# Layer 1's decode value rows: from split weights to raw float32 weights in four column groups

## The chip, the cores and the metric

The kernel runs on one core of one Trainium2 chip. The core has a matrix engine (PE in the profile; its weight loads are listed apart as PEld), a vector engine (DVE), a scalar engine (ACT), a general-purpose engine (POOL) and a queue that only issues DMAs (SP). [...] The metric is device time in microseconds (us), the median of several executions.

## The reference, cut to what matters

One inference step of two layers: a retention layer ("layer 1" here) and a sliding-window attention layer, for a prompt of 1024 positions and for 8 decode rows (one new token for each of 8 sequences). The change touches one product of layer 1, the value projection of the 8 decode rows:

```python
def retention_layer(x, S0, g_norm, w_in, g_out, w_out):
    B, L, _ = x.shape
    h = rmsnorm(x, g_norm)
    proj = h @ w_in                       # w_in: 1024 x 6144
    q, k, v, gate = jnp.split(proj, [RET_QK, 2 * RET_QK, 2 * RET_QK + RET_V], axis=-1)
    ...
    o, S = retention_scan(q, k, v, S0)    # S_t = gamma_h S_{t-1} + k_t^T v_t,  o_t = q_t S_t
    o = rmsnorm(o, g_out.reshape(RET_HEADS, RET_DV)).reshape(B, L, RET_V)
    o = o * jax.nn.silu(gate)
    return x + o @ w_out, S.astype(S0.dtype)
```

There are four heads, each with 512 value columns. So the product in question is, for each head, [8 x 1024] times [1024 x 512].

## The kernel before, in words

**The first stage** projects layer 1. The columns of the weight matrix are cut into 20 sets: for each head one query set and one key set of 256 columns and one value set of 512 columns, then eight gate sets of 256 columns. Each set is one matrix product of (prompt and decode rows) by (1024 x columns), done with a seven-product scheme of Strassen's kind: `SEQ7` names the seven weight operands A11, S2, S1, A12, S3, S4, A22, where the S are sums and differences of quarters of the weights. (The first two sets, the query and key sets of head 0, are done without the scheme.) Every product is done in a 3-term form: each operand is split into a high part in the type float32r (`hi`, `woh`, `xh`) and a remainder (`lo`, `wol`, `xl`), and hi*hi, hi*lo and lo*hi are added up in PSUM. `w_hi` (ACT, L216) and `w_lo` (DVE or POOL, L221) make the two weight parts, `w_sum` (POOL) the sums, from raw tiles of 128 x 1024 float32 (`raw`, five buffers, DMAs issued from ACT's queue, L181). A raw tile of a value set holds two blocks of 128 rows of the weights by 512 columns; four of them make a set.

**The order of work** is a plan: `prod_slot` makes one slot for each product and half of the prompt (`t` = 0, 1), so 14 slots for a set, each with an estimated time; their sum is a planned clock. PE's queue is the list of slots. The work of the other engines is put between slots in two ways: `later(n, ...)` at slot number n (evacuations of PSUM, spills to DRAM), and `when(t, ...)` at a planned time (raw loads, `w_sum`, `w_hi`, `w_lo` some microseconds before the product that needs them, and the steps of the decode rows' retention).

**Where the 8 decode rows go.** For query, key and gate sets the decode rows travel as two more columns of the moving operand (258 columns instead of 256). For value sets the weights are the moving operand and the prompt's positions the stationary one, so the decode rows have a product of their own, `vdec` (L334 to L344): the stationary operand is `xdecr` (the high parts of the 8 rows in columns 0 to 7, their remainders in columns 32 to 39) or `xdecd` (the same of a difference of two halves of the rows), 40 columns wide, the moving operand `woh` and then `wol` of A11, A12, S1 and A22, 256 columns each. Four times a value set, behind the slot with `t` = 1 of products 0, 2, 3 and 6, eight matmuls follow, into the PSUM tile `vd`. After the set `vout1` (ACT, L697) copies partitions 32 to 39 of `vd` into a ring buffer, `vout2` (DVE, L701) adds partitions 0 to 7, and SP writes the 8 x 512 values to the DRAM scratch `vscr` (L705). `xdec2_` and `xdec3_` (L502 to L508, four DVE operations and one POOL operation) prepare `xdecr` and `xdecd` while the first two sets run.

**The decode rows' retention.** From 10 us (planned) after the end of a value set, `dec_load` brings a piece of the recurrent state (L253) and the values from `vscr` to all partitions (L255), `dec_kv`, `dec_st`, `dec_y0`, `dec_y1` update it on ACT and DVE, and `dec_mm` (L277) sums over partitions on PE: four plain float32 matmuls with a stationary operand of 32 columns, each into its own 32 partitions of the PSUM tile `od`.

**After the first stage** come the chunked retention of the prompt (from L859 on), layer 1's output projection, and layer 2.

Of the kernel before, what the change touches and what calls it, by code (L numbers as in the profile page):

```python
# [7 lines left out]
F32 = mybir.dt.float32  # L8
# [8 lines left out]
ND = 8  # L17
# [53 lines left out]
def _trunk(ctx, tc, nc, a):  # L71
# [67 lines left out]
    xdecr = dcp.tile([128, 8, 40], F32R, name="xdecr")  # L139
    xdecd = dcp.tile([128, 4, 40], F32R, name="xdecd")  # L140
# [193 lines left out]
    def vdec(s, name):  # L334

        if name == "A11":
            s.pd = vdp.tile([128, 512], F32, name="vd")
        x, i, k0, first = {"A11": (xdecr, 0, 0, True), "A12": (xdecr, 0, 4, False),
                           "S1": (xdecr, 1, 0, True), "A22": (xdecd, 1, 0, False)}[name]
        dst = s.pd[0:40, 256 * i:256 * i + 256]  # L340
        for k in range(4):
            hi, lo = s.op[name, k // 2]
            mm(dst, x[:, k0 + k, :], hi[:, k % 2, :], start=(name == "A11" and k == 0), stop=False, skip_group_check=True)
            mm(dst, x[:, k0 + k, :], lo[:, k % 2, :], start=False, stop=(k == 3 and not first), skip_group_check=True)  # L344
# [57 lines left out]
    rdec = sp.tile([128, 8, ND], F32, name="rdec")  # L402
    rT = sp.tile([128, 7, 4, 4], F32, name="rT")
    rdif = sp.tile([128, 4, ND], F32, name="rdif")
# [95 lines left out]
    def xdec2_():  # L500

        dve.tensor_copy(xdecr[:, :, 0:8], rdec)  # L502
        dve.tensor_tensor(xdecr[:, :, 32:40], rdec, xdecr.bitcast(F32)[:, :, 0:8], SUB)
        pool.tensor_tensor(rdif, rdec[:, 4:8, :], rdec[:, 0:4, :], SUB)

    def xdec3_():
        dve.tensor_copy(xdecd[:, :, 0:8], rdif)
        dve.tensor_tensor(xdecd[:, :, 32:40], rdif, xdecd.bitcast(F32)[:, :, 0:8], SUB)  # L508

# [59 lines left out]
    def prod_slot(s, j, t):  # L569
        n = len(slots)  # L570
        name, x, b, first = SEQ7[j]
        dec = s.kind == "v" and t == 1 and j in (0, 2, 3, 6)

        def pe():
            if first:
                s.bk[b, t] = bank(b, t)
            product(s, s.bk[b, t], t, name, x, first)
            if dec:
                vdec(s, name)

        us = 2.84 if s.kind == "v" else 1.43
        slot((us + (0.95 if dec else 0.0)) * (1.045 if s is not sets[2] else 1.0), pe)
# [31 lines left out]
        [o(g1_open), o(th, T2, 5), o(t12, 7), o(tl, T2, 5), o(t34, 7), o(dsums, 0, (T4,)), o(xdec2_)],  # L614
        [o(th, T2, 7), o(th, T1, 5), o(tl, T2, 7), o(tl, T1, 5), o(xdec3_), o(dsums, 1, (T2,))],
# [1319 lines left out]
```

## Time and profile before

| | |
|---|---|
| median of 3 runs | 1350.39 us (1350.27 to 1351.85) |
| profiled execution, its own time | 1350.44 us |
| its span in the trace | 1348.6 us |
| granted PE clock, mean | 0.995 |
| busy: PE, PEld, DVE, ACT, POOL | 1308.8, 1222.4, 701.1, 633.6, 707.4 us |
| first stage's last product begins / chunked retention begins on PE | 539.7 us / 543.3 us |
| value sets of heads 0 to 3 begin on PE | 70.7, 155.6, 243.0, 330.5 us |

How to read the rows: a timeline row has the start, the duration, the engine, the line of the kernel, the operation, the tile written and the tiles read, the active part of the array (rows*columns), the shape, a count, and in brackets the idle time of the engine before it with what ended it. Matmuls overlap in a pipeline: one of 256 columns is shown as lasting 0.28 us, though the next one starts 0.12 us after it. So the cost of a matmul on PE is the distance between starts, not the duration. A plain float32 matmul leaves two records in the trace (64 such matmuls of `dec_mm` leave 128).

### The profile page before, as it was taken

What the parts mean: (1) busy time and instruction counts of PE and PEld (TensorE: products, weight loads), DVE (VectorE), ACT (ScalarE), POOL (GpSimd) and SP (SyncE); (2) the same over time, 40 slices, a digit from 0 to 9 for tenths busy, and PEclk for the clock granted to TensorE, in tenths of its full rate; (3) what the DMA queues carried; (4) which work ended last, traced back from release to release, by engine and by line L of the source; (5) the groups of instructions that cost most, each with busy time, mean ns of one, the idle gap of its engine ahead of it and who ended that gap; (6) DMA issues with size and microseconds to landing.
All of it is one profiled execution on the core that took longest, in us unless ns stands there. A gap on an engine that the chain in (4) does not pass through costs nothing.

```text
span 1348.6 us, 25951 instructions
## 1 busy us (share of the span) xinstructions
PE 1308.8 (97%) x9661; PEld 1222.4 (91%) x9661; DVE 701.1 (52%) x1365; ACT 633.6 (47%) x1565; POOL 707.4 (52%) x825
## 2 busy tenths in 40 slices
PE   6999999999999999899999999998999999999998
PEld 6999999999999999787877899997889999998998
DVE  6943655656566553676752113335456555669321
ACT  5532444544455553677751112235465656656321
POOL 6653534435435543698977545454375666555000
PEclk9999999999999999999999999999999999999999
DMA  6314777587676753556556434442121111113532
GB/s 221 103 55 140 218 222 225 161 242 233 187 237 187 233 177 107 169 171 212 182 160 196 153 121 136 143 119 72 38 62 44 48 46 46 34 34 107 159 86 80
DMA packets 194771, 187.68 MB, mean 139 GB/s; under 512 B 12645, under 2 KB 174493, under 8 KB 194629
## 3 DMA queue, kind: packets, MB, share of 16 engines
q1 hardware_dynamic: 156576, 147.29, 35.9%
q10 hardware_dynamic: 38068, 38.73, 9.1%
q8 instruction: 76, 1.25, 0.4%
q14 instruction: 51, 0.41, 0.1%
HBM read 129.61 MB, written 57.41 MB: 139 GB/s over the span
## 4 chain that ended last, share of the span: by engine, by line
PE 85%; DVE 5%; POOL 4%; issue 3%; DMA 2%; ACT 1%; ACTq 0%; SPq 0%; POOLq 0%; DVEq 0%
PE b L330 7%; PE b L332 7%; PE b L331 7%; PE pj L1132 7%; PE pj L1134 6%; PE pj L1133 6%; PE b L323 4%; PE b L324 4%; PE b L325 4%; PE tr L100 4%; PE pj L1181 4%; PE pj L1179 4%; PE pj L1180 4%; PE o L1600 2%; POOL wl L1122 1%
## 5 line engine op out<-in xcount | busy, mean ns | idle before, releaser
L330 PE MATMUL b<-xh,woh 128*128 128x258 f32 x784 | 223.3, 285 | 0.0
L332 PE MATMUL b<-xh,wol 128*128 128x258 f32 x784 | 221.6, 283 | 0.0
L331 PE MATMUL b<-xl,woh 128*128 128x258 f32 x784 | 221.2, 282 | 0.0
L1132 PE MATMUL pj<-A_hi,wh 128*128 128x384 f32 (+1 forms) x512 | 178.7, 349 | 0.0
L1134 PE MATMUL pj<-A_hi,wl 128*128 128x384 f32 (+1 forms) x512 | 165.2, 323 | 0.0
L1133 PE MATMUL pj<-A_lo,wh 128*128 128x384 f32 (+1 forms) x512 | 165.1, 323 | 0.0
L330 PEld LDWEIGHTS b<-xh,woh 128*128 128x128 f32 x784 | 148.0, 189 | 4.1 <-issue 2.5
L331 PEld LDWEIGHTS b<-xl,woh 128*128 128x128 f32 x784 | 148.8, 190 | 0.0
L332 PEld LDWEIGHTS b<-xh,wol 128*128 128x128 f32 x784 | 148.1, 189 | 0.0
L221 POOL TENSOR_TENSOR wol<-raw,woh 128x512 fp32r<-128x512 f32 x52 | 68.5, 1325 | 139.7 <-ACT woh L216 139.0
L1122 POOL TENSOR_TENSOR wl<-wr,wh 128x1024 fp32r<-128x1024 f32 (+1 forms) x60 | 114.2, 1913 | 40.2 <-DVE wh L1121 19.5
L324 PE MATMUL b<-wol,xh 128*128 128x256 f32 x448 | 126.1, 281 | 0.3 <-DVE wol L221 0.3
L323 PE MATMUL b<-woh,xh 128*128 128x256 f32 x448 | 126.3, 282 | 0.0
L325 PE MATMUL b<-woh,xl 128*128 128x256 f32 x448 | 125.7, 281 | 0.0
L1132 PEld LDWEIGHTS pj<-A_hi,wh 128*128 128x128 f32 x512 | 97.3, 190 | 10.1 <-issue 9.4
L1133 PEld LDWEIGHTS pj<-A_lo,wh 128*128 128x128 f32 x512 | 97.6, 191 | 0.0
L1134 PEld LDWEIGHTS pj<-A_hi,wl 128*128 128x128 f32 x512 | 97.0, 190 | 0.0
L1577 POOL TENSOR_TENSOR s<-s,sm 128x512 f32<-128x512 f32 x64 | 68.9, 1077 | 49.7 <-DVE sm L1576 47.8
L323 PEld LDWEIGHTS b<-woh,xh 128*128 128x128 f32 x448 | 84.4, 188 | 2.5 <-issue 1.2
L324 PEld LDWEIGHTS b<-wol,xh 128*128 128x128 f32 x448 | 84.3, 188 | 0.8 <-DVE wol L221 0.8
L325 PEld LDWEIGHTS b<-woh,xl 128*128 128x128 f32 x448 | 84.3, 188 | 0.0
L1569 ACT ACTIVATE s<-s,mx 128x257 f32<-128x257 f32 x128 | 64.3, 505 | 30.2 <-DVE mx L1567 26.4
(379 smaller groups left out, 3564.7 us busy)
## 6 DMA issues: line engine op xcount, KB each, us to landing
raw<-in_w_in_ret_dram ACTq DMA_DIRECT2D x44, 512.0 KB
st<-in_state_ret_dram SPq DMA_DIRECT2D x64, 256.0 KB
out_dram<-st SPq DMA_DIRECT2D x64, 256.0 KB
wr<-in_w_out_ret_dram SPq DMA_DIRECT2D x32, 512.0 KB
wr<-in_w_in_swa_dram SPq DMA_DIRECT2D x18, 512.0 KB
vb<-vscr SPq DMA_DIRECT2D x64, 128.0 KB
evp<-qks SPq DMA_DIRECT2D x32, 256.0 KB
evx<-vsc SPq DMA_DIRECT2D x32, 256.0 KB
```

The costliest lines, as they stand in the source:

```text
L221: eng.tensor_tensor(lo, src_of(s, name, sub), hi.bitcast(F32), SUB)
L323: mm(dst, xh, wh, start=a and i == 0, stop=False, skip_group_check=True)
L324: mm(dst, xh, wl, start=False, stop=False, skip_group_check=True)
L325: mm(dst, xl, wh, start=False, stop=z, skip_group_check=True)
L330: mm(dst, wh, xh, start=a, stop=False, **sg)
L331: mm(dst, wh, xl, start=False, stop=False, **sg)
L332: mm(dst, wl, xh, start=False, stop=z, **sg)
L1122: lo_eng[0].tensor_tensor(lo[:, js, :], raw[:, i:i + step, :], hi.bitcast(F32)[:, js, :], ALU.subtract)
L1132: mm(ps, hi[:, k, fs], xh[:, k, t0:t1], start=first and k == ks[0], stop=False)
L1133: mm(ps, hi[:, k, fs], xl[:, k, t0:t1], start=False, stop=False)
L1134: mm(ps, lo[:, k, fs], xh[:, k, t0:t1], start=False, stop=last and k == ks[-1])
L1577: nc.gpsimd.tensor_tensor(st[:, :, 0:256], st[:, :, 0:256], sm.unsqueeze(2).broadcast_to([128, 2, 256]), ALU.mult)
```

## The change

`vdec` is called once per value set, behind product 0 with `t` = 1, and no longer uses the split weights. It multiplies the 8 normalised decode rows in plain float32 (`rdec32`, 32 columns wide with 24 columns of zeros) by the raw weight tiles, 512 columns at a time. The eight blocks of 128 weight rows are eight matmuls. Block kt goes to the 32 partitions of `vd` that begin at 32 * (kt mod 4): blocks 0 to 3 start the four partial sums, blocks 4 to 7 are added to them. After the set the four partial sums (partitions 0 to 7, 32 to 39, 64 to 71, 96 to 103) are added on ACT and DVE: three copies and three additions instead of one of each. The write to `vscr` moves from slot n + 4 to n + 6 (n is the first slot of the next set). `xdecr`, `xdecd`, `rdif` and their five preparing operations go. The planned time of a value set's extra slots changes from four times 0.95 us to once 2.05 us, so all planned times behind it shift.

```diff
-    xdecr = dcp.tile([128, 8, 40], F32R, name="xdecr")
-    xdecd = dcp.tile([128, 4, 40], F32R, name="xdecd")
+    rdec32 = dcp.tile([128, 8, 32], F32, name="rdec")
+    rdec = rdec32[:, :, 0:ND]
...
-    def vdec(s, name):
-
-        if name == "A11":
-            s.pd = vdp.tile([128, 512], F32, name="vd")
-        x, i, k0, first = {"A11": (xdecr, 0, 0, True), "A12": (xdecr, 0, 4, False),
-                           "S1": (xdecr, 1, 0, True), "A22": (xdecd, 1, 0, False)}[name]
-        dst = s.pd[0:40, 256 * i:256 * i + 256]
-        for k in range(4):
-            hi, lo = s.op[name, k // 2]
-            mm(dst, x[:, k0 + k, :], hi[:, k % 2, :], start=(name == "A11" and k == 0), stop=False, skip_group_check=True)
-            mm(dst, x[:, k0 + k, :], lo[:, k % 2, :], start=False, stop=(k == 3 and not first), skip_group_check=True)
+    def vdec(s):
+
+        s.pd = vdp.tile([128, 512], F32, name="vd")
+        for kt in range(8):
+            j, sub, kk, g = kt // 4, kt % 4 // 2, kt % 2, kt % 4
+            mm(s.pd[32 * g:32 * g + 32, :], rdec32[:, kt, :], s.raw[2 * sub + j][:, kk, :], start=(kt < 4), stop=(kt >= 4))
+
+    def vsum1(s, g):
+        s.vt = ring("c")[0:ND, 0:512]
+        act(s.vt, s.pd[32 * g:32 * g + ND, :], AF.Copy)
+
+    def vsum2(s, g):
+        if g == 1:
+            s.vs = ring("w")[0:ND, 0:512]
+        dve.tensor_tensor(s.vs, s.pd[0:ND, :] if g == 1 else s.vs, s.vt, ADD)
...
-        dec = s.kind == "v" and t == 1 and j in (0, 2, 3, 6)
+        dec = s.kind == "v" and t == 1 and j == 0
...
-                vdec(s, name)
+                vdec(s)
...
-        slot((us + (0.95 if dec else 0.0)) * (1.045 if s is not sets[2] else 1.0), pe)
+        slot((us + (2.05 if dec else 0.0)) * (1.045 if s is not sets[2] else 1.0), pe)
...
-            later(n + 1, vout1)
-            later(n + 2, vout2)
-            later(n + 4, lambda s=s: nc.sync.dma_start(out=vscr[s.h], in_=s.vs))
+            for g in (1, 2, 3):
+                later(n + g, vsum1, s, g)
+                later(n + g + 1, vsum2, s, g)
+            later(n + 6, lambda s=s: nc.sync.dma_start(out=vscr[s.h], in_=s.vs))
```

On PE, behind the first product of head 0's value set (`b` is the product's PSUM tile, `woh` and `wol` the split weights), the queue had before:

```order
L325 MATMUL b_985<-woh,xl 128x256
L343 MATMUL vd<-woh,xdecr 40x256
L344 MATMUL vd<-wol,xdecr 40x256
L343 MATMUL vd<-woh,xdecr 40x256
L344 MATMUL vd<-wol,xdecr 40x256
L343 MATMUL vd<-woh,xdecr 40x256
L344 MATMUL vd<-wol,xdecr 40x256
L343 MATMUL vd<-woh,xdecr 40x256
L344 MATMUL vd<-wol,xdecr 40x256
L323 MATMUL b_1034<-woh,xh 128x256
```

and now has, at the same place:

```order
L324 MATMUL b_976<-wol,xh 128x256
L325 MATMUL b_976<-woh,xl 128x256
L339 MATMUL vd<-raw,rdec 32x512 x8
L323 MATMUL b_1025<-woh,xh 128x256
L324 MATMUL b_1025<-wol,xh 128x256
```

Eight matmuls of 256 columns became eight of 512; the three other groups of eight in the set are gone. In head 2 the eight stand directly ahead of a group of `dec_mm` (L277), with no full-width matmul between them.

On DVE, while the first two sets run and up to the first two `wol` of head 0's value set (L476, L486, L487 split the prompt's operands), the queue had before:

```order
L502 CAST xdecr<-rdec 128x8x8
L503 TENSOR_TENSOR xdecr<-rdec,xdecr 128x8x8
L476 TENSOR_TENSOR xl<-raw,xh 128x4x128
L476 TENSOR_TENSOR xl<-u,xh 128x4x128
L507 CAST xdecd<-rdif 128x4x8
L508 TENSOR_TENSOR xdecd<-rdif,xdecd 128x4x8
L486 CAST xh<-rT 128x4x2
L487 TENSOR_TENSOR xl<-rT,xh 128x4x2
```

and now has (the lines' numbers are two higher):

```order
L478 TENSOR_TENSOR xl<-raw,xh 128x4x128
L478 TENSOR_TENSOR xl<-u,xh 128x4x128
L488 CAST xh<-rT 128x4x2
L489 TENSOR_TENSOR xl<-rT,xh 128x4x2
L478 TENSOR_TENSOR xl<-raw,xh 128x4x128
```

Four operations went from ahead of those `wol`; the order of the others is the same.

On DVE at the start of head 1's query set (`evp`, `evx`, `evw` are ring buffers that take the evacuated products), the queue had before:

```order
L701 TENSOR_TENSOR evw<-vd,evc 8x512
L361 TENSOR_TENSOR evp<-b_1486,evp 128x258
L361 TENSOR_TENSOR evp<-b_1503,evp 128x258
L221 TENSOR_TENSOR wol<-s_1484,woh 128x512
L363 TENSOR_TENSOR evx<-b_1521,evp 128x258
```

and now has:

```order
L348 TENSOR_TENSOR evw<-vd,evc 8x512
L348 TENSOR_TENSOR evw<-evw,evc 8x512
L365 TENSOR_TENSOR evp<-b_1453,evp 128x258
L348 TENSOR_TENSOR evw<-evw,evc 8x512
L365 TENSOR_TENSOR evp<-b_1472,evp 128x258
L221 TENSOR_TENSOR wol<-s_1451,woh 128x512
```

Two more additions stand ahead of the next `wol`; on ACT two more copies (L343) stand among the evacuations of the same slots.

More of the change, by code (lines that the diff above doesn't have):

```diff
@@ L766, in _trunk @@
         pool.memset(oneh[:, r, r:r + 1], 1.0)
-    pool.memset(xdecr.bitcast(F32), 0.0)
-    pool.memset(xdecd.bitcast(F32), 0.0)
+    pool.memset(rdec32, 0.0)
     nc.scalar.dma_start(out=gb, in_=norm_ret[0].partition_broadcast(128))
```

19 lines of the change are left out of this document (2 added, 17 removed).

## The prediction

> **What bounds the kernel now.** I read the page first, then the windows table, the table of waits, and last the timeline at the lines that the change touches. The page has the span and PE's share of it:
>
> ```profile
> span 1348.6 us, 25951 instructions
> PE 1308.8 (97%) x9661; PEld 1222.4 (91%) x9661; DVE 701.1 (52%) x1365; ACT 633.6 (47%) x1565; POOL 707.4 (52%) x825
> ```
>
> PE is busy 97% of the span, but the share is a mean over stages; the change lies in the first stage. The windows table for the stretch from shortly after the first value set's start to the stage's end (length, busy time of PE, PEld, DVE, ACT and POOL with counts, granted clock):
>
> ```profile
> 78.00:543.00 465.00, 464.76 (x3916) 455.22 (x3913) 247.65 (x432) 214.96 (x470) 207.86 (x243) 1.00 0.63 190
> ```
>
> PE is busy for 464.76 of 465 us at full clock, the other engines about half. The table of waits, for PE in the same stretch, consists of its heading alone:
>
> ```profile
> engine line waited for: us in total, times, longest us
> ```
>
> So PE waits for nobody there. A matmul more or less in this stretch is time more or less, at the distance between starts. The decode rows' value product is such work. One group of eight, from the timeline of PE:
>
> ```profile
> 77.26 0.28 PE L343 MATMUL vd<-woh,xdecr 128*40 128x256 f32 x1
> 77.38 0.28 PE L344 MATMUL vd<-wol,xdecr 128*40 128x256 f32 x1
> ...
> 78.08 0.28 PE L344 MATMUL vd<-wol,xdecr 128*40 128x256 f32 x1
> 78.20 0.28 PE L323 MATMUL b<-woh,xh 128*128 128x256 f32 x1
> ```
>
> The group takes PE from 77.26 to 78.20: 0.94 us, or 0.1175 for each matmul of 256 columns, whatever the width of its weights.
>
> **The change: what goes on PE.** The groups by line, from the view of line 343:
>
> ```profile
> L343 PE MATMUL vd<-woh,xdecr x48: 276/281/283, 77.3 to 356.6; 128*40 128x256 f32 x48
> L343 PE MATMUL vd<-woh,xdecd x16: 278/279/284, 114.2 to 375.3; 128*40 128x256 f32 x16
> ```
>
> That is 64, and each has a partner on line 344: 128 matmuls, 16 groups of eight. 16 x 0.94 = 15.0 us leave PE, 3.76 for each of the four value sets. All 16 lie in the stretch without waits, or at its edge.
>
> **What comes on PE.** For each value set eight plain float32 matmuls, 32 weight columns, 512 moving columns, in four column groups. Before has nothing of this size, but it has the same form with 256 columns: `dec_mm`, four plain float32 matmuls into four 32-partition groups of one PSUM tile, each with a moving tile of its own. Its view by line, and then one call in the timeline:
>
> ```profile
> L277 PE MATMUL od<-yd,oneh x128: 379/391/403, 158.5 to 495.5; 128*32 128x256 f32 x128
> ```
>
> ```profile
> 158.29 0.28 PE L325 MATMUL b<-woh,xl 128*128 128x256 f32 x1
> 158.49 0.64 PE L277 MATMUL od<-yd,oneh 128*32 128x256 f32 x8
> 159.06 0.38 PE L323 MATMUL b<-woh,xh 128*128 128x256 f32 x1
> 159.28 0.28 PE L324 MATMUL b<-wol,xh 128*128 128x256 f32 x1
> ```
>
> Each float32 matmul leaves two records (passes, I will say), so the four leave eight. A record lasts 0.38 to 0.40 us, and all eight together last 0.64: the four groups run at the same time, and what is left is two rounds, one for each pass. The price of the whole call: from the L325 at 158.29 to the L324 at 159.28 are 0.99 us; without the call the two starts behind that L325 would take 2 x 0.1175 = 0.235. So 0.755 us.
>
> To carry this to 512 columns I have to split it into rounds and a fixed part. The price of a pass without column groups stands in the next stage, four records (two float32 matmuls) of 128 columns, with a float32r matmul of 512 columns ahead:
>
> ```profile
> 549.45 0.40 PE L924 MATMUL po<-vh,sTl 128*128 128x512 f32 x1
> 549.68 0.61 PE L859 MATMUL tr<-evp 128*128 128x128 f32 x4
> 550.13 0.38 PE L100 MATMUL tr<-ident,evp 128*128 128x128 f32 x2
> ```
>
> From 549.68 to 550.13 are 0.45 us for four: 0.1125 for 128 columns, so 0.225 for 256 and 0.45 for 512. Two rounds of 256 are 0.45; of the 0.755 there remain 0.305, which is the cost of going into the narrow groups and out again, once for a call. [...]
>
> For a value set: blocks 0 to 3 are two rounds, blocks 4 to 7, added to the same partitions, two more. 4 x 0.45 + 0.305 = 2.105 us; four sets 8.4 us. The gain on PE is 15.0 - 8.4 = 6.6 us. From both sides: a pass of 512 can be a little cheaper than four of 128 (L924's 512 columns take 0.23 where 256 take 0.1175, 1.96 times), which makes a round 0.44 and the four sets 0.16 us cheaper or more; the fixed part may be half as large (0.6 us cheaper over the sets) or twice as large (1.2 dearer). In head 2 the order puts a `dec_mm` right behind the eight, so one way in and one way out of the narrow groups can fall away together: between 0 and 0.3 us more; I take 0.15.
>
> **The start of the first value set.** There PE does wait, for the remainders `wol` of the first operand:
>
> ```profile
> 70.72 0.28 PE L323 MATMUL b<-woh,xh 128*128 128x256 f32 x1
> 71.33 0.39 PE L324 MATMUL b<-wol,xh 128*128 128x256 f32 x1 [0.34 <-DVE wol L221]
> 71.55 0.29 PE L325 MATMUL b<-woh,xl 128*128 128x256 f32 x1
> ...
> 72.74 0.28 PE L323 MATMUL b<-woh,xh 128*128 128x256 f32 x1
> 73.02 0.38 PE L324 MATMUL b<-wol,xh 128*128 128x256 f32 x1
> 73.25 0.28 PE L325 MATMUL b<-woh,xl 128*128 128x256 f32 x1
> ```
>
> Twice two steps of 0.1175 became longer: 0.83 - 0.235 and 0.51 - 0.235, together 0.87 us. The `wol` come late because DVE works through its queue without a gap up to them:
>
> ```profile
> 63.24 0.18 DVE L502 CAST xdecr<-rdec 128x64 fp32r<-128x64 f32 x1
> ...
> 63.60 0.69 DVE L476 TENSOR_TENSOR xl<-raw,xh 128x512 fp32r<-128x512 f32 x1
> ...
> 64.81 0.17 DVE L507 CAST xdecd<-rdif 128x32 fp32r<-128x32 f32 x1
> ...
> 65.13 1.19 DVE L486 CAST xh<-rT 128x8 fp32r<-128x8 f32 x1
> ...
> 68.08 0.16 DVE L486 CAST xh<-rT 128x8 fp32r<-128x8 f32 x1
> ...
> 70.59 2.38 DVE L221 TENSOR_TENSOR wol<-raw,woh 128x512 fp32r<-128x512 f32 x2
> ```
>
> The four operations that go took 63.60 - 63.24 = 0.36 and 65.13 - 64.81 = 0.32, so the `wol` can come 0.68 us earlier. How much of it arrives is not certain: the same L486 lasts 0.16 or 1.19 us, so DVE is slowed by something else here, and a shift can change that. Bounds: all 0.87 saved, or 0.3 lost; I take 0.5, near the 0.68.
>
> **The sums behind the set.** Two copies on ACT and two additions on DVE come on top in each head:
>
> ```profile
> L697 ACT ACTIVATE evc<-vd x4: 589/590/591, 115.3 to 375.8; 8x512 f32<-8x512 f32 x4
> L701 DVE TENSOR_TENSOR evw<-vd,evc x4: 672/672/677, 116.0 to 376.6; 8x512 f32<-8x512 f32 x4
> ```
>
> 2 x 0.59 + 2 x 0.67 = 2.5 us per head. I cost them at nothing on PE. The cover, at the start of head 1's query set: two DVE rows behind the new additions, an evacuation and a split, and the PE row that first needs that `wol` (fifth product of the set):
>
> ```profile
> 119.74 0.43 DVE L361 TENSOR_TENSOR evp<-b,evp 128x258 f32<-128x258 f32 x1 [3.09 <-PE b L332]
> 121.54 0.68 DVE L221 TENSOR_TENSOR wol<-s,woh 128x512 fp32r<-128x512 f32 x1
> 126.69 0.29 PE L330 MATMUL b<-xh,woh 128*128 128x258 f32 x1
> ```
>
> DVE stands idle for 3.09 us just where 1.34 us are added, and the `wol` is ready at 122.22, 4.5 us before PE wants it. If that cover were gone, a head would cost up to 2.5 us.
>
> The write to `vscr` stands two slots later and behind three sums; SP's queue behind it holds `dec_load` of head 0 and the spills. SP's two rows and the first reader of the values on ACT:
>
> ```profile
> 116.67 0.29 SPq L705 DMA_DIRECT2D vscr<-evw  x1
> 118.28 0.40 SPq L255 DMA_DIRECT2D vb<-vscr  x1
> 130.07 0.90 ACT L260 ACTIVATE kv<-vb,kd 128x256 f32<-128x256 f32 x2
> ```
>
> The write may go some 3 to 4 us later (two query slots of about 1.45 us, and the sums), so `vb` is asked for at 122 instead of 118.28, and is wanted at 130: hidden. The other heads begin their decode steps later than 10 us after their set. Four of the eight matmuls wait for the DMA of a raw tile; the weight sums for the next product are planned 9 to 13 us ahead of it and read all four tiles, so these waits are over before PE comes to them. The raw tiles now have PE as one more reader, behind product 0; their last reader is still a sum on POOL for product 4 or a split for product 6, so the loads do not move for that.
>
> **Sum.** 6.6 + 0.15 + 0.5 = 7.25 us. The profiled execution took 1350.44 (0.05 above the median of the runs, so no correction): 1350.44 - 7.25 = 1343.2 us.
>
> **The rivals.** *Two passes in strict order (4%).* If a matmul's two passes stand one behind the other in PE's queue and no matmul starts before the one ahead of it, then a group overlaps only the second pass of one block with the first of the next: nine rounds for eight blocks, 9 x 0.45 + 0.305 = 4.36 us instead of 3.76, 2.4 us more over the sets, less the 0.65 of the two small terms: 1352.2. [...] Against it speaks the `od` row: in strict order its four would need five rounds, the last starting 4 x 0.225 = 0.9 us after the first, and the call would last 0.9 + 0.38 = 1.28 us instead of 0.64.
>
> *The groups do not overlap at 512 columns (4%, the other sign).* Four streams of 512 float32 into one PSUM tile could be held up where four of 256 from small tiles are not. With no overlap at all the eight cost 16 x 0.45 + 0.305 = 7.5 us, 3.74 more than now, 15.0 over the sets: 1350.44 + 15.0 - 0.65 = 1364.8. The point from which the change is a loss is 3.76 us for the eight, 7.7 rounds instead of 4. Nothing in the trace speaks for it; `od` fills a tile of four groups in the same way.
>
> *The gain is given back (6%).* PE arrives 7 us earlier at the end of the stage and could wait there for decode work or read-backs, giving 1350. Against it: the last `od` record starts at 495.5, and the next stage begins long after that:
>
> ```profile
> 543.33 0.68 PE L859 MATMUL tr<-evp 128*128 128x128 f32 x4 [0.56 <-issue]
> ```
>
> That is 48 us of slack for the decode rows, and the read-backs for the next stage are placed ten slots before the stage's end and move with it.
>
> **How the numbers follow.** A measurement of this kernel can tell about 0.2%, 2.7 us, from no change. The forecast has 86%. Its own range: 5.1 us of gain (fixed part doubled, 0.3 lost at the start, nothing in head 2) to 8.5 (rounds of 0.44, half the fixed part, 0.87 at the start, 0.3 in head 2): 1341.9 to 1345.3. The rivals hold 14%, so this range with 0.3 us of room on either side, 1341.6 to 1345.6, holds about 8 in 10. Faster by over 0.2%: 0.87 (the forecast, and a strong remainder of a partial give-back). Within 0.2%: 0.08 (strict order, most of the give-back). Slower: 0.05 (no overlap, or sums that surface).
>
> **What would show it.** In the new profile each value set should show one row of 16 records of `vd`, about 2.1 us from the last full-width start ahead to the normal rhythm behind; records of one round starting within some 0.03 us of one another, rounds 0.45 apart. The gap in front of the first `wol` of head 0 should be about gone. The table of waits for PE from 78 us to the stage's end should still be its heading alone, and the next stage should begin near 536. Starts of `vd` records spread evenly over 4 us or more would prove strict order or no overlap; rows of PE waiting for `wol` or `woh` in the query sets behind the value sets would prove that the sums are not hidden.

## The result, and the profile after

| | before | after |
|---|---|---|
| median (lowest to highest), 13 runs each, side by side | 1350.39 us (1348.51 to 1352.52) | 1347.49 us (1346.07 to 1349.89) |
| ratio, 95% interval | | 0.9978 (0.997 to 0.9987) |
| profiled execution, its span | 1350.44, 1348.6 us | 1346.37, 1344.6 us |
| retention begins on PE | 543.33 us | 535.78 us |
| from there to the end of the span | 805.28 us | 808.79 us |

The change gains 2.9 us where 7.25 were forecast, and the median lies 1.9 us above the range. In later comparisons the same two kernels are 5.2 and 6.6 us apart, so the gain is real and its size scatters. The last two rows of the table say where to look: the first stage became 7.55 us shorter, and the work behind it, which the change does not touch, 3.5 us longer.

The page of after, its span and its busy times:

```profile
span 1344.6 us, 25813 instructions
PE 1304.7 (97%) x9597; PEld 1213.1 (90%) x9597; DVE 709.6 (53%) x1369; ACT 636.2 (47%) x1573; POOL 710.1 (53%) x823
```

PE has 64 records fewer; that number returns below. The windows table of the first stage (length, busy time of PE, PEld, DVE, ACT, POOL with counts, granted clock, DMA share, GB/s):

```profile
70.00:78.00 8.00, 8.00 (x72) 7.24 (x74) 5.82 (x7) 4.46 (x9) 4.80 (x6) 1.00 0.07 19
78.00:536.00 458.00, 457.43 (x3854) 443.36 (x3843) 254.91 (x438) 218.57 (x479) 211.26 (x243) 1.00 0.64 193
```

PE is busy without a break, also from 70 to 78 us, where it waited before; the 0.57 us missing in the second row stand in front of the next stage. The table of waits for PE from 78 to 535.5 us is its heading alone again, so PE does not wait for the additional sums on ACT and DVE. The new product in the timeline of PE, head 0:

```profile
76.75 0.28 PE L325 MATMUL b<-woh,xl 128*128 128x256 f32 x1
76.96 1.92 PE L339 MATMUL vd<-raw,rdec 128*32 128x512 f32 x16
78.81 0.39 PE L323 MATMUL b<-woh,xh 128*128 128x256 f32 x1
79.04 0.28 PE L324 MATMUL b<-wol,xh 128*128 128x256 f32 x1
```

The sixteen passes together last 1.92 us. From the L325 at 76.75 to the L324 at 79.04 are 2.29 us; less two steps of 0.118, the set's decode product costs 2.05 us. And the first row of the next stage:

```profile
535.78 0.68 PE L843 MATMUL tr<-evp 128*128 128x128 f32 x4 [0.57 <-issue]
```

The stage came out close to the forecast (7.55 us for 7.25). What failed lies after 536 us, and in the time from which the gain was subtracted.

### The profile page after: what moved, and what is told of

It is laid out like the page before. It is cut to its first block, busy times and chain, and to the rows that moved or that the text cites. A ratio compares the mean times of both kernels' runs of the same rounds, so it can differ in the third digit from the quotient of the medians.

```text
span 1344.6 us, 25813 instructions
## 1 busy us (share of the span) xinstructions
PE 1304.7 (97%) x9597; PEld 1213.1 (90%) x9597; DVE 709.6 (53%) x1369; ACT 636.2 (47%) x1573; POOL 710.1 (53%) x823
## 4 chain that ended last, share of the span: by engine, by line
PE 86%; POOL 4%; DVE 3%; DMA 3%; issue 2%; ACT 2%; SPq 0%; ACTq 0%; POOLq 0%; DVEq 0%
PE b L330 7%; PE b L331 7%; PE b L332 7%; PE pj L1116 7%; PE pj L1117 6%; PE pj L1118 6%; PE b L323 4%; PE b L324 4%; PE b L325 4%; PE tr L100 4%; PE pj L1165 4%; PE pj L1163 4%; PE pj L1164 4%; PE o L1584 2%; PE b L537 2%
## 5 line engine op out<-in xcount | busy, mean ns | idle before, releaser
L324 PE MATMUL b<-wol,xh 128*128 128x256 f32 x448 | 126.0, 281 | 0.0
L325 PE MATMUL b<-woh,xl 128*128 128x256 f32 x448 | 125.6, 280 | 0.0
L325 PEld LDWEIGHTS b<-woh,xl 128*128 128x128 f32 x448 | 84.3, 188 | 0.0
L324 PEld LDWEIGHTS b<-wol,xh 128*128 128x128 f32 x448 | 84.3, 188 | 0.0
```

The lines of the kernel that those rows point to most:

```text
L324: mm(dst, xh, wl, start=False, stop=False, skip_group_check=True)
L325: mm(dst, xl, wh, start=False, stop=z, skip_group_check=True)
```

## Theories

**Theory A, blocks of instructions.** The trace lists among the DMA packets some of the kind "instruction", of 16 KB each in one queue:

```profile
q8 instruction: 76, 1.25, 0.4%
```

That is 76 packets for PE's 9597 records. Around 710 us they come 24 to 31 us apart, and between two of them PE has 113 to 129 matmul records; over the whole trace of after the middle value is 127 (91 to 163). So I take these to be PE's instructions, about 128 records (with their weight loads) in a block. The change takes 64 records out of PE's program, half a block, and every later packet falls half a block later in the work. Behind the first stage one of them then collides with a load that PE waits for.

**Theory B, the early arrival.** PE comes 7.5 us earlier to work whose loads do not come earlier by as much.

**Theory C, chance.** In the traces the granted clock falls to 0.50 for windows of 3.41 us, in other places in each execution: at 706.6, 921.6, 948.9 and 1259.5 us in before, at 698.9, 893.5, 910.6, 944.7 and, two in a row, 1006.1 us in after, and in both once more in the last microsecond. By this theory the forecast compared a lucky execution with ordinary ones.

The place for A and B: the stretch on PE from the first `S<-ident,xr` to the first `tr<-ident,kd`, layer 1's output projection and the beginning of layer 2. Before, then after:

```profile
706.70 1.09 PE L100 MATMUL S<-ident,xr 128*128 128x128 f32 x4 [3.12 <-DMA xr<-in_x_prompt_dram]
897.32 0.59 PE L100 MATMUL tr<-ident,kd 128*128 128x128 f32 x2 [0.15 <-DVE kd L1321]
```

```profile
698.88 1.04 PE L100 MATMUL S<-ident,xr 128*128 128x128 f32 x4 [3.03 <-DMA xr<-in_x_prompt_dram]
891.98 0.59 PE L100 MATMUL tr<-ident,kd 128*128 128x128 f32 x2 [1.00 <-DVE kd L1305]
```

It takes 190.62 us before and 193.10 after. Of the 3.5 us, 2.5 lie in this stretch and 1.3 behind it; ahead of it after is 0.3 us quicker. In the stretch PE waits for the remainder `wl` (POOL) of a projection weight; the chain behind it is `wh` (DVE) and the load of `wr` (issued by SP). Before, the timeline rows of that chain:

```profile
722.29 0.37 SPq L1114 DMA_DIRECT2D wr<-in_w_out_ret_dram  x1
726.06 1.11 DVE L1121 CAST wh<-wr 128x1024 fp32r<-128x1024 f32 x1 [2.67 <-DMA wr<-in_w_out_ret_dram]
729.69 0.50 PE L1181 MATMUL pj<-A_hi,wl 128*128 128x512 f32 x1 [0.46 <-POOL wl L1122]
```

and after:

```profile
714.30 0.37 SPq L1098 DMA_DIRECT2D wr<-in_w_out_ret_dram  x1
720.32 0.69 DVE L1105 CAST wh<-wr 128x1024 fp32r<-128x1024 f32 x1 [4.85 <-DMA wr<-in_w_out_ret_dram]
723.50 0.50 PE L1165 MATMUL pj<-A_hi,wl 128*128 128x512 f32 x1 [1.70 <-POOL wl L1106]
```

The same load comes 3.8 us after its issue before, and 6.0 us after it now; DVE waits for it 2.2 us longer and PE 1.2 us longer. The DMA view of after, first for 714.2 to 720.4 us, then for 717.9 to 719.1 us alone:

```profile
q8 instruction: 1, 0.02, 1.0%
```

```profile
DMA packets 71, 0.04 MB, mean 33 GB/s; under 512 B 10, under 2 KB 71, under 8 KB 71
```

One instruction packet lies between issue and landing (it starts at 717.15 us in the trace and lasts 0.95), and behind it the sixteen DMA engines together move 33 GB/s for 1.2 us, about a tenth of the 313 GB/s from 717 to 718 us: their busy share in the windows table falls from 1.02 to 0.14 while the rest of the load is still out. Before, the same view for 722.2 to 726.2 us has no instruction packet and a mean of 258 GB/s. Which of the sixteen engines were still at work is not shown.

The second place is 886 us, where SP and ACT issue small loads that the `kd` rows need. Before, then after:

```profile
891.89 0.81 SPq L1741 DMA_DIRECT2D xr<-xscr  x2
892.68 0.46 ACTq L1272 DMA_DIRECT2D kgb<-in_k_norm_dram  x1
```

```profile
885.97 1.82 SPq L1725 DMA_DIRECT2D xr<-xscr  x2
886.47 1.32 ACTq L1256 DMA_DIRECT2D kgb<-in_k_norm_dram  x1
```

In after an instruction packet starts at 886.38; the issues on both queues take 1.0 and 0.9 us longer, and PE waits 1.00 us for `kd` at the end of the stretch, where it waited 0.15 before.

## Experiments

Unless said otherwise, a run was timed beside the kernel before; the medians of before in these comparisons were 1351.43, 1352.35, 1353.26 and 1352.75 us.

**e1_before_again and e2_after_again** are the two kernels unchanged.

> The kernel before, unchanged, for a second trace and for the scatter of one against itself. The two traces at hand show the first stage shorter by 7.5 us (the chunked retention begins at 535.8 instead of 543.3), as the change's terms say, and the span shorter by 4.0 only: 3.5 us come back between 543 us and the end, where the two programs are the same. Theory chance: the part behind the first stage varies from execution to execution by a few us (half-speed windows of the granted clock, late DMAs), and the trace of before was a lucky one; then this trace has a first stage of 543.3 +-0.5 and a rest that differs from 805.3 us by 1 us or more, towards longer. Theory shift: the rest depends on when the first stage ends; then the rest is 805.3 +-0.7 again. The timed ratio is 1.000 +-0.001 by either.

> The changed kernel, unchanged, for a second trace. Theory chance: the first stage ends at 535.8 +-0.5, and the rest differs from the 808.8 us of its first trace by 1 us or more, towards shorter. Theory shift: the rest is 808.8 +-0.7 again. Ratio 0.998 by the runs so far.

Before: 1352.07 us, ratio 0.9999 (0.9989 to 1.001). After: 1346.23 us, ratio 0.9962 (0.995 to 0.9975). The retention began at 543.53 and 535.68 us, the stretch took 190.93 and 192.47 us. So both numbers belong to the kernels; the total gain, 5.2 us this time instead of 2.9, does so less. Nor does the whole rest from the start of the retention to the end of the span, on which the two expectations were built: it took 805.3 and 805.9 us in the profiles of before, 808.8 and 807.2 in those of after, and by itself the second value of after would have spoken for chance. That is why the stretch, and not the rest, is compared from here on.

**e3_product_twice** issues the new product twice for each value set.

```diff
-        s.pd = vdp.tile([128, 512], F32, name="vd")
+        if not hasattr(s, "pd"):
+            s.pd = vdp.tile([128, 512], F32, name="vd")
...
                 vdec(s)
+                vdec(s)
```

> The changed kernel with the eight column-group matmuls of each value set issued twice (the second eight compute the same values again). The second eight need no way in and out of the narrow groups, so they should cost four rounds of 0.43 us: 1.72 us a set, 6.9 in all, and the first stage should end at 542.7. Theory chance: the rest keeps its mean, the total is 1347.5 + 6.9 = 1354.4. Theory shift (what follows depends on when the first stage ends, and not on the kernel): the first stage ends where before's does, so the total is before's, 1350.4 +-0.7.

1351.78 us, ratio 1.0006 (0.9995 to 1.0017). The retention begins at 542.55 us, 6.8 us later than in the two profiles of after. In the timeline of PE:

```profile
76.94 3.64 PE L340 MATMUL vd<-raw,rdec 128*32 128x512 f32 x32
80.51 0.39 PE L323 MATMUL b<-woh,xh 128*128 128x256 f32 x1
```

The second product adds 3.64 - 1.92 = 1.72 us, four rounds of 0.43; the way into the narrow groups and out is paid once. The stage follows PE's work to a tenth of a microsecond. But the total rose by 5.5 us over e2, and the stretch went back to 190.93 us: the kernel has 9661 records again, like before.

**e4_before_half_product** leaves out half of the old decode product, two of its four groups of eight.

```diff
-            if dec:
+            if dec and j in (0, 2):
```

> The kernel before with two of the four groups of eight decode-row matmuls of each value set left out (those on A12 and A22, so half of each sum is missing from the decode rows' values); sums, evacuations, plan and everything else stay. PE has 64 matmuls of 0.1175 us less: the first stage should end at 543.3 - 7.5 = 535.8, as in the changed kernel. Theory chance: the rest keeps its mean, the total is 1350.4 - 7.5 = 1342.9. Theory shift: the total is the changed kernel's, 1347.5 +-0.7, since the first stage ends at the same time. Rival, the changed kernel's own doing (its rest is longer for something it does, not for the time at which it starts): 1342.9 here too, and 1354.4 with the product twice.

1348.26 us, ratio 0.9973 (0.9962 to 0.9984). The retention begins at 535.90 us, 7.4 earlier, for eight groups of 0.94. The stretch takes 192.90 us. So the longer stretch is not the new product's doing: this kernel, which does not have it, has 9597 records and an early retention too. A and B both allow that.

**e5, e6, e7 and e8** tell A from B. They put tiny matmuls into the time at the start in which PE waits for its first load (32 of them in e5 and e8, 64 in e6, 16 in e7; each leaves two records). The 64 of e6 last until 8.1 us, somewhat longer than that wait, but its first value set begins at 70.75 us, no later than the others.

```diff
+    pad = vdp.tile([128, 512], F32, tag="vd", name="pad")
+    for k in range(32):
+        mm(pad[0:32, 0:8], oneh[:, 0, :], oneh[:, 1, 0:8], start=True, stop=True)
```

In PE's timeline of e7 (16 matmuls) they end long before the load:

```profile
1.11 1.87 PE L772 MATMUL pad<-oneh 128*32 128x8 f32 x32 [1.11 <-POOL oneh L751]
7.33 0.99 PE L100 MATMUL pd<-ident,u 8*128 8x8 f32 x8 [4.35 <-DMA ident<-const_c_dram]
```

> The changed kernel with 32 tiny plain float32 matmuls (64 records, 8 columns each) put ahead of PE's first work; their result is overwritten unused. PE waits there until 7.5 us, so the retention should still begin on PE at 535.8 us. The stretch from the retention's last part to layer 2's norm (PE rows S<-ident,xr to tr<-ident,kd, near 700 to 890 us) took 190.6 to 190.9 us in the three runs with 9661 PE records and 192.5 to 193.1 in the three with 9597. Theory A, blocks of instructions: PE's instructions are fetched in packets of 16 KB (one every 128 records); 64 records fewer put one such packet between issue and landing of the wr load that PE waits for. 64 records more bring the packet back to where it was in the kernel before: 190.5 to 191.0 us, PE's gap at the wl wait 0.9 instead of 2.1, and a time 2 us below that of the changed kernel, 1344.5. Theory B, the earlier arrival itself collides with the loads: 192.5 to 193.1, 1346.5. Windows of half clock add 0 to 3 us to any single run.

> The same with 64 tiny matmuls, 128 records: one whole packet of instructions. Theory A: the packets fall on the same work as in the changed kernel, so the stretch is 192.5 to 193.1 us again and the time 1346.5, that is 2 us above the run with 64 records. Theory B: the same 192.5 to 193.1. A value near 190.7 would speak against both and for the extra records as such.

> The same with 16 tiny matmuls, 32 records: a quarter of a packet. Theory A: the packet that came at 717.1 us comes about 7 us earlier, near 710, ahead of the issue of the critical wr load at 714.3; the stretch is then 190.5 to 191.5 us and the time 1344.5 to 1345.5. Theory B: 192.5 to 193.1 and 1346.5.

> The kernel before with the same 32 tiny matmuls ahead, 64 records. The retention begins at 543.4 us as before. Theory A: the packet that came at 708.8 us comes near 695 and the next one near 723, between issue (722.3) and landing (726.1) of the wr load: the stretch becomes 192.5 to 193.1 us instead of 190.7 and the time 1352.5 to 1353.5, 2 us above the kernel before. Theory B: late arrival, so 190.6 to 190.9 and no change of time.

| | records | retention begins | packets in the stretch's first 40 us | stretch | median | ratio (95%) |
|---|---|---|---|---|---|---|
| e5, after + 64 | 9661 | 535.19 us | +2.1, +31.0 us | 191.21 us | 1345.76 us | 0.9951 (0.9939 to 0.9964) |
| e6, after + 128 | 9725 | 535.34 | +19.1 | 195.12 | 1347.43 | 0.9965 (0.9953 to 0.9977) |
| e7, after + 32 | 9629 | 535.56 | +11.8, +37.8 | 190.74 | 1344.07 | 0.9939 (0.9924 to 0.9954) |
| e8, before + 64 | 9725 | 543.28 | +17.9 | 194.04 | 1354.21 | 1.0011 (0.9999 to 1.0023) |

In the two profiles shown the packets come +18.3 us (after) and +2.1, +30.5 us (before) behind the start of the stretch. B falls: e5 and e7 begin the retention as early as after and have the short stretch, and e8 begins it as late as before and has the long one. A holds in all four, and e6, where a whole block was added, is long again. The clock, the other candidate, does not make the difference either: all profiles but three have one window of half clock at the start of the stretch, e11 and e13 (below) a second one near 726 us; of the three without any, e5 and e14 have 191.2 and 191.1 us and e10, with a packet in the way, has 192.4. The chain of the `wr` load in e7, e6 and e8:

```profile
716.16 0.37 SPq L1101 DMA_DIRECT2D wr<-in_w_out_ret_dram  x1
719.91 1.15 DVE L1108 CAST wh<-wr 128x1024 fp32r<-128x1024 f32 x1 [2.64 <-DMA wr<-in_w_out_ret_dram]
723.58 0.50 PE L1168 MATMUL pj<-A_hi,wl 128*128 128x512 f32 x1 [0.67 <-POOL wl L1109]
```

```profile
722.88 0.69 DVE L1108 CAST wh<-wr 128x1024 fp32r<-128x1024 f32 x1 [4.75 <-DMA wr<-in_w_out_ret_dram]
726.06 0.51 PE L1168 MATMUL pj<-A_hi,wl 128*128 128x512 f32 x1 [1.69 <-POOL wl L1109]
```

```profile
727.94 0.69 DVE L1124 CAST wh<-wr 128x1024 fp32r<-128x1024 f32 x1 [4.11 <-DMA wr<-in_w_out_ret_dram]
731.12 0.50 PE L1184 MATMUL pj<-A_hi,wl 128*128 128x512 f32 x1 [1.67 <-POOL wl L1125]
```

The sizes fit less well than the places: e5 was expected at 1344.5 us and came 1.3 higher, and e8 is above before by 1.9 us of medians, with an interval that still holds 1. The stretches of e6 and e8, 195.12 and 194.04 us, are longer than the 192.5 to 193.1 that was expected. Among the waits of PE from 690 to 900 us (total, times, longest) after has one wait for `wl`, e6 has three and one for `wh` (e8 has two for `wl`, 2.3 us together). After, then e6:

```profile
PE pj L1165 <- POOL wl L1106: 1.7, 1, 1.7
```

```profile
PE pj L1168 <- POOL wl L1109: 2.7, 3, 1.7
PE pj L1166 <- DVE wh L1108: 0.4, 1, 0.4
```

The longest is the same 1.7 us.

**e9_one_column_group and e10_neighbours_in_one_group** test the price of the new product. In e9 all eight blocks go to one column group, in e10 two neighbours go to the same one.

```diff
-            j, sub, kk, g = kt // 4, kt % 4 // 2, kt % 2, kt % 4
-            mm(s.pd[32 * g:32 * g + 32, :], rdec32[:, kt, :], s.raw[2 * sub + j][:, kk, :], start=(kt < 4), stop=(kt >= 4))
+            j, sub, kk, g = kt // 4, kt % 4 // 2, kt % 2, 0
+            mm(s.pd[32 * g:32 * g + 32, :], rdec32[:, kt, :], s.raw[2 * sub + j][:, kk, :], start=(kt == 0), stop=(kt == 7))
...
-        act(s.vt, s.pd[32 * g:32 * g + ND, :], AF.Copy)
+        act(s.vt, s.pd[0:ND, :], AF.Copy, scale=0.0)
```

```diff
-            j, sub, kk, g = kt // 4, kt % 4 // 2, kt % 2, kt % 4
-            mm(s.pd[32 * g:32 * g + 32, :], rdec32[:, kt, :], s.raw[2 * sub + j][:, kk, :], start=(kt < 4), stop=(kt >= 4))
+            j, sub, kk, g = kt // 4, kt % 4 // 2, kt % 2, kt // 2
+            mm(s.pd[32 * g:32 * g + 32, :], rdec32[:, kt, :], s.raw[2 * sub + j][:, kk, :], start=(kt % 2 == 0), stop=(kt % 2 == 1))
```

> The changed kernel with all eight blocks of vd in one column group (partitions 0 to 31, one running sum); the three copies behind it read that sum times 0, so their work and PE's instructions stay. If the four groups at the same time are what makes the new product cheap, its 16 passes now follow one another at 0.43 us: per set 16 x 0.43 instead of 4 x 0.43, 5.16 us more, so the retention begins on PE at 535.6 + 20.6 = 556.2 us. If something else made it cheap (shorter passes), the start stays near 536.

> The changed kernel with blocks 0 and 1 in the first column group, 2 and 3 in the second, and so on: the same 16 passes, but four in a row go to the same group. If a pass that must wait for its group lets the passes behind it go ahead, the order makes no difference: four rounds, the retention at 535.6 us. If it holds up all that stand behind it, the last pass of a group and the first of the next start together: 13 rounds, 9 x 0.43 = 3.9 us more per set, the retention at 551.1 us. Values between would tell how many passes can wait.

The retention begins at 556.06 us in e9 and at 535.58 us in e10 (one run each: 1366.82 and 1348.89 us). PE's row of the product, e9 and then e10:

```profile
76.80 7.05 PE L339 MATMUL vd<-raw,rdec 128*32 128x512 f32 x16
```

```profile
76.68 1.95 PE L339 MATMUL vd<-raw,rdec 128*32 128x512 f32 x16
```

Without the groups the sixteen passes follow one another at 0.43 us and the set costs 7.18 us; the whole of the cheapness is the four groups at the same time. Written in e10's order the price is nearly the same: the sixteen starts form four rounds 0.43 us apart, the four of a round within 0.04 us, and the set costs 2.07 us where after has 2.05. As passes for one group follow one another (e9), the four of a round must belong to four groups. So in e10 four passes in a row for the same group do not hold up the other groups, and PE does not start these matmuls in the order in which they are written. Started strictly in the written order, e10 would have had 13 rounds and begun the retention at 551 us, as its expectation works out; it began 15.5 us earlier.

**e11_split_rows_kept** brings back the preparation of the split decode rows, whose results nobody reads. The diff is cut to the first of its two calls.

```diff
...
-        [o(g1_open), o(th, T2, 5), o(t12, 7), o(tl, T2, 5), o(t34, 7), o(dsums, 0, (T4,))],
+        [o(g1_open), o(th, T2, 5), o(t12, 7), o(tl, T2, 5), o(t34, 7), o(dsums, 0, (T4,)), o(xdec2_)],
...
```

> The changed kernel with the preparation of the split decode rows kept (the four DVE operations of xdec2_ and xdec3_ and the subtraction on POOL, whose results nobody reads). If the wait for the first set's wol went with these operations, as the prediction has it, the gap before the first L324 of head 0 comes back (0.3 us and the second step of 0.28, 0.87 us over both) and the retention begins 0.3 to 0.9 us later than the 535.6 us of the changed kernel. If it went for another reason, the gap stays away and the start stays at 535.2 to 535.8.

The retention begins at 535.73 us (1349.99 us in one run). The first value set in e11, and in after:

```profile
70.92 0.28 PE L325 MATMUL b<-woh,xh 128*128 128x256 f32 x1
71.18 0.39 PE L326 MATMUL b<-wol,xh 128*128 128x256 f32 x1
71.40 0.28 PE L327 MATMUL b<-woh,xl 128*128 128x256 f32 x1
```

```profile
71.19 0.28 PE L323 MATMUL b<-woh,xh 128*128 128x256 f32 x1
71.31 0.28 PE L324 MATMUL b<-wol,xh 128*128 128x256 f32 x1
```

The four DVE operations bring back one gap: the start of the set up to the decode product takes 5.98 us, where after has 5.77 and before 6.54. So they account for 0.21 of the 0.77 us, in one profile; what removed the rest is open. The set itself begins between 70.60 and 71.19 us in the profiles, whatever the kernel, which is more than that.

**e12_before_32_records_ahead** gives before the shift of e7.

> The kernel before with 16 tiny matmuls ahead (32 records), the shift that made the changed kernel 1344.07 us. If the gain there was that a packet of instructions left the way of the loads, nothing is to be had here, where no packet stood in their way: the packet of 708.8 us comes near 701.6, the next near 730, the stretch stays at 190.6 to 191.2 us and the time at the kernel before, ratio 0.999 to 1.001. If the tiny matmuls as such help (a warmer start), the kernel before gains as much as the changed one did, 2 to 3 us, ratio 0.998.

1352.15 us, ratio 0.9996 (0.9981 to 1.0011); the stretch takes 190.38 us, its packet at +23.9 us. The tiny matmuls as such bring nothing.

**e13_after_third_time and e14_after_32_records_again** put after and e7's kernel side by side.

> The changed kernel once more. By theory A (a packet of PE's instructions in the way of the wr load and of the issues near 886 us) the stretch between S<-ident,xr and tr<-ident,kd takes 192.4 to 193.2 us, the retention begins at 535.2 to 535.8, and the time is 4 to 5 us below the kernel before (ratio 0.9963 to 0.997). If all that is missing is chance, the stretch scatters between 190.5 and 193.2.

> The changed kernel with 16 tiny matmuls (32 records) ahead once more, beside the changed kernel in the same call. Theory A: the stretch takes 190.5 to 191.3 us, PE's wait for wl about 0.7 us instead of 1.4 to 1.7, and the median lies 1.5 to 3 us below the changed kernel's, at a ratio to before of 0.994 to 0.9955. Chance alone: the two medians lie within 1 us.

After: 1346.14 us, ratio 0.9952 (0.9935 to 0.997), stretch 194.21 us, PE's `wl` wait 1.7 us. With 32 records: 1345.37 us, ratio 0.9957 (0.9938 to 0.9976), stretch 191.07 us. The stretches lie on the sides that A gives them, though that of after is longer than expected (it has the second window of half clock). Two things missed. PE's waits for `wl` with 32 records were to be 0.7 us and are

```profile
PE pj L1168 <- POOL wl L1109: 1.9, 2, 1.2
```

so this wait alone does not tell the two kinds of profile apart. And the medians lie 0.8 us apart, not 1.5 to 3; less than 1 us was what chance alone was to give. The scatter of single runs (1342.79 to 1350.03 us) covers the difference, and this is theory C.

## Chance: the granted clock

In the profile of after the clock is half for two windows in a row from 1006 us on. The same matmuls in PE's timeline of after, ahead of these windows and inside:

```profile
1000.80 0.34 PE L1116 MATMUL pj<-A_hi,wh 128*128 128x384 f32 x1
1000.97 0.34 PE L1117 MATMUL pj<-A_lo,wh 128*128 128x384 f32 x1
...
1009.71 0.53 PE L1116 MATMUL pj<-A_hi,wh 128*128 128x384 f32 x1
1010.03 0.53 PE L1117 MATMUL pj<-A_lo,wh 128*128 128x384 f32 x1
```

Starts 0.17 us apart become 0.32 us. The windows table has the clock of 1004 to 1012 us in after, and in e2, which is the same kernel:

```profile
1004.00:1012.00 8.00, 6.47 (x29) 5.71 (x30) 2.92 (x8) 4.53 (x11) 6.86 (x9) 0.63 0.47 155
```

```profile
1004.00:1012.00 8.00, 7.11 (x55) 6.63 (x55) 3.76 (x9) 5.95 (x15) 7.06 (x10) 1.00 0.52 158
```

29 records against 55 in the same 8 us. Behind the start-up every profile has five to eight such windows (before five, after seven), one of them in the last microseconds, their starts multiples of 3.41 us apart (63, 8 and 91 times 3.41 us between the first four of before), and the grid lies differently in each execution. In the traces of before and after the granted clock is 0.50 inside them and 1.00 outside. Most come at or shortly behind a stretch in which PE waits (near 700, 900 to 950, 1006 and 1255 us; the longest wait there is 0.4 to 3.1 us in before and 1.0 to 3.0 in after), but not behind the same waits each time. What sets them off is not shown.

Each timed run has its mean granted clock. A straight line through the 187 runs of all kernels that have one (a constant for each kernel, one slope) gives 0.60 +- 0.04 us for each microsecond of (1 - clock) x 1348, with 1.3 us left over. This is a correlation: no run sets the clock, and the runs come from several sets on several chips. At equal clock, and against before:

| kernel | records | packet in the way | difference to before (standard error) |
|---|---|---|---|
| after (25 runs) | 9597 | yes | -5.6 us (0.3) |
| after + 32 (13 runs) | 9629 | no | -7.3 (0.4) |
| after + 64 | 9661 | no | -6.6 (0.6) |
| after + 128 | 9725 | yes | -4.8 (0.6) |
| half the old product | 9597 | yes | -5.0 (0.4) |
| product twice | 9661 | no | -0.1 (0.4) |
| before + 32 | 9693 | no | -0.1 (0.4) |
| before + 64 | 9725 | yes | +1.8 (0.4) |

The column in the middle is from the traces. Of sixteen profiles, nine have a packet 16.5 to 19.1 us behind the start of the stretch; their stretches take 191.56 to 195.12 us, those of the other seven 190.38 to 191.21. PE's wait for `kd` at the end of the stretch is 0.69 to 1.45 us in the nine and 0.13 to 0.26 in the seven. The lowest of the nine is e9, with the earliest of these packets: its `wr` load was not late (PE's wait for `wl` is 0.5 us), only its issues near 905 us were. At equal clock the packet costs 1.7 us (after against after + 32, standard error 0.5 us) and 1.8 us (before + 64 against before, 0.4 us). Two comparisons give less: after against after + 64 has 0.9 us (0.6), and e13 against e14 alone, side by side, 0.9 us (0.6). So the sign is clear and the size is 1 to 2 us. And the kernel whose packets are out of the way gains 7.3 us, close to the forecast's sum.

## Why the prediction was wrong, point by point

- **What goes: 16 x 0.94 = 15.0 us.** Measured from the starts in the traces of before: 15.02. Right.
- **What comes: 2.105 us a set.** 2.05 in heads 0, 1 and 3, 1.72 in head 2; 7.87 in all for 8.25 forecast (8.4 less 0.15). A round is 0.43, not 0.45, and the way in and out is 0.33 us; head 2 saves the whole of it. From the first `vd` record to the next stage it was 466.07 us before and 458.83 after, in every profile of the two kernels, padded or not, within 0.01: 7.24 us where 6.75 were forecast.
- **The start of the first value set: 0.5 us.** The part up to the decode product shrank by 0.77. The size was within the bounds; the reason was mostly not the one given, since bringing the four operations back cost 0.21. Together the stage's two terms gave 8.0 us for 7.25; that the retention begins only 7.55 us earlier is because the first value set begins 0.47 us later in this profile (71.19 for 70.72 us). The closeness of 7.55 to 7.25 is in part luck.
- **The sums cost nothing.** Right on PE, which waits for nobody in the stage. But their size on DVE was wrong: the two additional additions were costed at 0.67 us each, like the one that was there, and take nearly twice that. The view of line 348 in after:

```profile
L348 DVE TENSOR_TENSOR evw<-evw,evc x8: 1141/1272/1781, 116.2 to 374.1; 8x512 f32<-8x512 f32 x8
L348 DVE TENSOR_TENSOR evw<-vd,evc x4: 672/672/673, 114.4 to 370.0; 8x512 f32<-8x512 f32 x4
```

  The eight read both operands from ring buffers and ran while POOL worked on the weights for most or all of the time; the four read `vd` and ran while POOL stood idle, but for 0.07 us. Which of the two makes them slow was not tried. The cover was large enough.
- **Strict order, no overlap.** Neither happens; e9 shows the price that no overlap would have had, 20.4 us on the stage, where the prediction had 15.0 over before (28.14 against 15.02 in the starts: 13.1).
- **The step that failed first: the Sum, "1350.44 - 7.25", by which a gain on PE's first stage reaches the end whole.** The rival "the gain is given back" had 6% and was looked for at the end of the stage, in waits for decode work. The stage has no such wait. About 1.7 us (0.9 to 1.8 by the comparisons above) go behind it, at two places 180 and 350 us later: taking 64 records out of PE's program moves the packets of its instructions against the work (+2.1 and +30.5 us behind the start of the stretch in before, +18.3 in after), one of them into the way of a load that PE was already waiting for, and one in front of the issues at 886 us. Nothing in the diff is near there, and order and instructions behind the stage are the same. The trace of before did show it: the stretch had a wait for `wl` (0.46 us, no slack) and packets of instructions among its DMAs.
- **The second step that failed: "no correction" to the profiled execution.** It had a granted clock of 0.995, where the 76 later runs of before have 0.993 in the mean and 1352.6 us; the 13 runs of after had 0.9923. By the slope that is 0.60 x 0.0027 x 1348 = 2.2 us. 1343.2 + 1.7 + 2.2 = 1347.1, and 1347.49 was measured. The 2.2 us rest on the correlation alone. That the 13 runs of before beside them were as lucky (mean 1350.65 us, where the later sets of before had 1352.3 to 1352.9) can't be shown from their clock, which is not on record for them; it would explain why the ratio was 0.9978 there and 0.9952 and 0.9962 later.

That the sum comes out is no proof of its parts. What the runs show is that the place of the packets lengthens the stretch; that the rest of the shortfall is the clock is argued.

What stays open: why the load comes 2.2 us later when the packet itself takes 0.95 us, and why the issues on SP's and ACT's queues become longer while a packet is on its way. The late load was seen in eight of the nine profiles and the long issues in seven; neither is explained.

The best version is the changed kernel with 32 records ahead: 0.9939 (0.9924 to 0.9954) and 0.9957 (0.9938 to 0.9976) of before. It beats before clearly; against the changed kernel it is 1.7 us better at equal clock over all runs and 0.8 us in the one pair of medians. The padding works for this program length alone: with 32 records fewer (after) or 96 more (e6) a packet is in the way again; with 32 more (e5) it is not.

## What to carry to other kernels

A gain on a busy PE arrives whole at the end of its stage where the stage has no waits (within a tenth of a microsecond in e3 and e4), but it reaches the end only if the waits behind it stay as they are; before the sum is carried over, list those waits and what stands close to them, instruction packets among it: here 32 records more moved a packet from +18.3 to +11.8 us behind the start of the stretch (after, e7). Where 0.2% is at stake, compare at equal granted clock, and try a padding of a quarter and a half block of instructions (32 and 64 records here) in idle time before believing a small loss or gain. The small float32 product with 32 weight columns was cheap in four column groups: sixteen passes of 512 columns for 2.05 and 2.07 us in the two orders that were tried, where one group took 7.18.

## What was not expected of the hardware

- The trace lists packets of the kind "instruction", taken here for PE's, of 16 KB each among those of the DMA engines that move the data: 76 for 9597 matmul records, one for about 128. A packet takes 0.96 us in the middle of after (0.88 to 1.58) and 0.98 in before (0.88 to 1.65). In after one between a load's issue and its landing went with a 512 KB load that came 2.2 us later; one at the time of an issue went, in seven of nine profiles, with an issue of 1.2 to 1.8 us instead of 0.4 to 0.5.
- A plain float32 pass of 512 columns takes 0.43 us (the distance between starts in e9), 0.1075 for each 128 columns, and in e10 passes for other column groups went ahead of passes written before them (four rounds 0.43 us apart, not 13).
- A microsecond that the granted clock counts as lost goes with 0.60 us of time in the 187 runs, a correlation; that the rest falls where PE would have waited anyway is a guess, and was not tried.
